# Four of the eight experts on 64 places each, with the low and the high part of a token side by side

## The chip, the core and the metric

The kernel runs on one core of a Trainium2 chip. TensorE (PE) multiplies, VectorE (DVE) and ScalarE (ACT) work on tiles, GpSimd (POOL) does little here, and SyncE (SP) issues the loads from HBM. The metric is the time of one execution on the device in microseconds; the median of three runs of the kernel before is 2383.63 us (2382.58 to 2390.08).

## The reference, cut to what matters

Two blocks of two layers each run over 256 tokens of width 1024. The last layer's feed-forward part is a mixture of eight experts, and it alone is touched by the change:

```python
logits = (t @ w_router) + b_router
top_v, top_i = lax.top_k(logits, 2)
top_w = softmax(top_v)
combine = sum(one_hot(top_i, 8) * top_w[..., None], axis=1)
for e in range(8):
    y += combine[:, e:e+1] * ((silu(t @ w1[e]) * (t @ w3[e])) @ w2[e])
```

w1 and w3 are 1024 x 2816, w2 is 2816 x 1024, all float32: 34.6 MB an expert. With the inputs as they are drawn (seed 0) the reference's router gives the eight experts 56, 59, 87, 61, 48, 82, 40 and 79 tokens, 512 in all.

## The kernel before

A float32 product is made from rounded parts: `split` (lines 417 to 419) lets ACT write the high part of a number (a cast) and DVE the low part (a subtraction), and `mm3` (lines 392 to 397) adds three products: high by high, high by low, low by high. Weights are loaded in units of 1 MB (128 x 2048) by `unit` and `raw` (lines 356 to 381) into a ring of five buffers, `raw`; each unit is then split in two halves of 128 x 1024 into `whi` (five buffers) and `wlo` (four). A load can start when both halves of the unit that held its buffer are split.

`moe` (line 1788) computes the router's logits, ranks the experts of a token, and counts on PE (lines 1841 to 1845) the place that a token takes in each of its two experts. `moe_round` (line 1877) then takes the experts in four pairs. For a pair it builds one-hot tiles `oh` from the places (line 1894), gathers the tokens of both experts with products by `oh` into `gh` and `gl` (high and low part, 128 places an expert), runs `expert` twice, and adds both results to the tokens through the transposed one-hot `ohT` (line 1928). This stretch between two experts of different pairs is called the boundary below.

`expert` (line 1932) goes over 11 blocks of 256 columns. A block takes three units: e1, e3 (eight row blocks of 128 x 256 each) and e2. It has 48 products of 256 columns into `ps_mm`, a SiLU on ACT, a product on DVE, two transposes, a split into `eph` and `epl`, and 12 products of 512 columns into `ps_acc`; the latter run one block late (`pend`).

All engines take their instructions in order, and a scheduler wrote that order from estimates of its own. If an expert had over 128 tokens, the code behind `tc.If` (line 1871) would run all experts once more.

Of the kernel before, what the change touches and what calls it, by code (L numbers as in the profile page):

```python
# [127 lines left out]
def _consts():  # L128
# [33 lines left out]
    c['tri8'] = np.broadcast_to(tri.reshape(1, 64), (P, 64))  # L162
    return {k: np.ascontiguousarray(v, dtype=np.float32).reshape(P, -1) for k, v in c.items()}
# [12 lines left out]
def pack(I):  # L176
# [30 lines left out]
    for e in range(NE):  # L207
        A[f'e1_{e}'] = _colblocks(I['exp_w1_2'][0, e])
        A[f'e3_{e}'] = _colblocks(I['exp_w3_2'][0, e])
        A[f'e2_{e}'] = _rowunits(I['exp_w2_2'][0, e])  # L210
# [74 lines left out]
class Kern:  # L285
# [1489 lines left out]
    def moe_consts(self, pw):  # L1775
        self.xw = pw
        self.pad(pw, 64)
        wr = pw.tile([P, KC * NE], F32, name="wr")
        self.nc.sync.dma_start(wr, self.a['wr'])
        lt = self.sm.tile([P, S], F32, tag="sq", bufs=2, name="ltf")[:, :P]  # L1780
        self.nc.sync.dma_start(lt, self.const_ap('lt'))
        ltb, oneb = pw.tile([P, P], BF, name="ltb"), pw.tile([P, P], BF, name="oneb")
        self.nc.vector.tensor_copy(ltb, lt)
        self.nc.vector.memset(oneb, 1.0)
        self.route = (wr, self.row(pw, 'brout'), self.c(pw, 'tri8'), ltb, oneb,
                      self.c(pw, 'iota'))

    def moe(self):
# [3 lines left out]
        with self.stage("moe") as pl:  # L1792
# [6 lines left out]
            wr, br, tri8, ltb, oneb, iota = self.route  # L1799
# [48 lines left out]
            tt(pos, pos, pp[:, 0:2 * NE].rearrange("p (t e) -> p t e", t=NT), op=ALU.add)  # L1848
            cnt = pl.tile([P, 1], F32, name="cnt")
            nc.vector.tensor_reduce(cnt, pp[:, 2 * NE:3 * NE], AX.X, ALU.max)  # L1850
# [16 lines left out]
            tiles = [tkh, tkl, pos, weights]  # L1867
            self.moe_round(pl, tiles, iota)
            self.final(pl)
            mx = nc.values_load(cnti[0:1, 0:1], min_val=0, max_val=S)  # L1870
            with tc.If(mx > P):

                ts(pos, pos, -float(P), None, op0=ALU.add)
                self.moe_round(pl, tiles, iota)
                self.final(pl)

    def moe_round(self, pl, tiles, iota):
# [5 lines left out]
        gate = self.mcol(1, 5, 0)  # L1883
        for e0 in range(0, NE, 2):
# [7 lines left out]
            for e in range(2):  # L1892
                for t in range(NT):
                    ts(oh[:, t, e], iota, pos[:, t, e0 + e:e0 + e + 1], None, op0=ALU.is_equal)
            gh = pl.tile([P, KC, 2 * P], F32R, tag="gh", name=self.nm("gh"))
            gl = pl.tile([P, KC, 2 * P], F32R, tag="gl", name=self.nm("gl"))
            for k in range(KC):
# [5 lines left out]
                nc.scalar.copy(gh[:, k], pg[:, 0:S])  # L1903
                nc.vector.tensor_copy(gl[:, k], pg[:, S:2 * S])
            if callable(tiles[3]):
                tiles[3] = tiles[3]()
            comb = tiles[3]
# [11 lines left out]
            ys = []  # L1919
            self.rings = [r for r in self.rings if r[0] is not self.xw and r[1] != "raw2"] + [(pl, "raw2", 1)]  # L1920
            for e in range(2):
                ys.append(self.expert(pl, e0 + e, (gh, gl), e, wsl[:, e:e + 1]))
            for m in range(KC):
                pm = self.psum("mx")
                n = 0
                for e in range(2):
                    for y in ys[e]:
                        nc.tensor.matmul(pm[:, :S], y[:, m * P:(m + 1) * P], ohT[:, e], start=n == 0, stop=n == 3)
                        n += 1
                self.resid(m, pm[:, :S], gate)  # L1930

    def expert(self, pl, e, g, t, wcol):
# [3 lines left out]
        def tail(fb, p):  # L1936
# [6 lines left out]
            w = self.blkunit(f'e2_{e}', fb, 2)  # L1943
# [6 lines left out]
        for fb in range(NF // 2):  # L1950
            w1 = self.blkunit(f'e1_{e}', fb, KC)
            pm = self.psum()
            self.proj_tm(pm[:, 0:256], w1, 0, 256, g, t)
            w3 = self.blkunit(f'e3_{e}', fb, KC)
# [7 lines left out]
        tail(*pend)  # L1962
        y = self.xw.tile([P, 2, D], F32R, tag=("xa", "xb")[t], name=self.nm("ey"))
# [58 lines left out]
```

## Time and profile before

| | |
|---|---|
| median of three runs | 2383.63 us |
| the profiled execution, and its span | 2392.68 us, 2390.8 us |
| busy in the span: PE, DVE, ACT | 2288.4, 1932.4, 1371.7 us |
| read from HBM | 515.55 MB, 216 GB/s over the span |
| loads of expert weights | 264 of 1 MB, the first issued at 1402.2 us, the last at 2335.8 us |

A view in stretches gives busy time by engine, with the number of instructions in brackets, the granted clock of TensorE (1.00 is 2.4 GHz), the busy share of the 16 DMA engines and the GB/s that they moved. In the order of time, a row of x3 is three instructions in one piece; its second number is the length of the whole piece. PE's instructions overlap: what one costs is the distance of starts, not its duration.

### The profile page before, as it was taken

The numbers are of one execution on the slowest core, as the hardware profiler recorded it, in microseconds if no ns is written. First come the engines' busy times: TensorE is split into PE (matmuls) and PEld (weight loads), VectorE is DVE, ScalarE is ACT, GpSimd is POOL, SyncE is SP. The second block draws the span as 40 slices with busy tenths as digits, with TensorE's granted clock in tenths as the row PEclk, the third lists the DMA queues.
The fourth block names the chain that finished last, engine by engine and source line by source line (L and its number), as shares of the span: only waits on it lengthen the run. The fifth ranks groups of instructions, "written<-read, shape, count | busy, mean of one in ns | idle before, by whom it ended". The sixth has DMA issues, their size and how long they took to land.

```text
span 2390.8 us, 41817 instructions
## 1 busy us (share of the span) xinstructions
PE 2288.4 (96%) x16477; PEld 2128.6 (89%) x16477; DVE 1932.4 (81%) x3447; ACT 1371.7 (57%) x2186; POOL 37.2 (2%) x40
## 2 busy tenths in 40 slices
PE   7999998999999999999999999989999999999998
PEld 7999998989998888888888898879999989999997
DVE  7879996768997886797657567779989998998996
ACT  6655554655544656432223246568877777876775
POOL 1000000000000000000000000000000000000000
PEclk9999998999998999999999999999999999999998
DMA  6335663534665231254655223269989998998992
GB/s 230 140 121 219 232 229 134 180 140 160 238 239 205 71 124 55 94 213 182 219 176 213 82 89 107 73 247 358 367 307 368 363 367 305 359 367 302 366 364 86
DMA packets 77453, 519.38 MB, mean 217 GB/s; under 512 B 10400, under 2 KB 12832, under 8 KB 15552
## 3 DMA queue, kind: packets, MB, share of 16 engines
q1 hardware_dynamic: 77248, 516.63, 58.9%
q8 instruction: 131, 2.15, 0.4%
q14 instruction: 74, 0.61, 0.1%
HBM read 515.55 MB, written 1.05 MB: 216 GB/s over the span
## 4 chain that ended last, share of the span: by engine, by line
PE 86%; DVE 8%; ACT 2%; issue 2%; DMA 2%; POOL 0%; SPq 0%; DVEq 0%; ACTq 0%; POOLq 0%
PE ps_mm L395 15%; PE ps_mm L396 15%; PE ps_mm L397 15%; PE ps_acc L395 7%; PE ps_acc L396 7%; PE ps_acc L397 7%; PE ps_mx L395 3%; PE ps_mx L397 3%; PE ps_mx L396 3%; DVE wlo L419 2%; PE ps_mx L472 2%; PE ps_acc L1532 1%; PE ps_acc L1355 1%; PE ps_mx L1901 1%; DMA raw<-wmod 1%
## 5 line engine op out<-in xcount | busy, mean ns | idle before, releaser
L418 ACT CAST whi<-raw 128x1024 fp32r<-128x1024 f32 x875 | 900.9, 1045 | 463.7 <-PE ps_mm L397 137.7
L419 DVE TENSOR_TENSOR wlo<-raw,whi 128x1024 fp32r<-128x1024 f32 x875 | 1047.9, 1214 | 138.0 <-ACT whi L418 49.0
L396 PE MATMUL ps_mm<-wlo,gh 128*128 128x256 f32 x1408 | 391.6, 279 | 4.1 <-DVE wlo L419 4.1
L395 PE MATMUL ps_mm<-whi,gh 128*128 128x256 f32 x1408 | 394.0, 280 | 0.0
L397 PE MATMUL ps_mm<-whi,gl 128*128 128x256 f32 x1408 | 390.5, 278 | 0.0
L396 PEld LDWEIGHTS ps_mm<-wlo,gh 128*128 128x128 f32 x1408 | 264.3, 188 | 11.0 <-DVE wlo L419 5.7
L397 PEld LDWEIGHTS ps_mm<-whi,gl 128*128 128x128 f32 x1408 | 265.3, 189 | 5.7
L395 PEld LDWEIGHTS ps_mm<-whi,gh 128*128 128x128 f32 x1408 | 264.4, 188 | 1.7
L395 PE MATMUL ps_mm<-hhi,whi 128*128 128x256 f32 (+2 forms) x544 | 154.7, 284 | 23.0 <-ACT whi L418 15.0
L397 PE MATMUL ps_mm<-hhi,wlo 128*128 128x256 f32 (+2 forms) x544 | 153.9, 283 | 2.2 <-DVE wlo L419 2.1
L396 PE MATMUL ps_mm<-hlo,whi 128*128 128x256 f32 (+2 forms) x544 | 153.6, 282 | 1.6 <-DVE hlo L424 1.1
L395 PE MATMUL ps_mm<-whi,hhi 128*128 128x256 f32 x480 | 139.0, 290 | 6.3 <-DVE rot L515 3.4
L396 PE MATMUL ps_acc<-wlo,eph 128*128 128x512 f32 x352 | 139.0, 395 | 0.0
L1071 DVE SCALAR_TENSOR_TENSOR raw<-raw,cond 128x1024 f32<-128x1024 f32 x96 | 115.9, 1219 | 28.3 <-DMA raw<-wmod 27.8
L396 PE MATMUL ps_mm<-wlo,hhi 128*128 128x256 f32 x480 | 137.4, 287 | 0.0
L397 PE MATMUL ps_mm<-whi,hlo 128*128 128x256 f32 x480 | 137.1, 287 | 0.0
L395 PE MATMUL ps_acc<-whi,eph 128*128 128x512 f32 x352 | 135.4, 403 | 1.5 <-ACT eph L418 1.5
L397 PE MATMUL ps_acc<-whi,epl 128*128 128x512 f32 x352 | 132.1, 397 | 0.0
L395 PEld LDWEIGHTS ps_mm<-hhi,whi 128*128 128x128 f32 (+2 forms) x544 | 100.2, 184 | 25.0 <-ACT whi L418 15.4
L397 PE MATMUL ps_acc<-hhi,wlo 128*128 128x256 f32 x368 | 104.3, 284 | 1.4 <-DVE wlo L419 1.4
L396 PE MATMUL ps_acc<-hlo,whi 128*128 128x256 f32 x368 | 104.2, 284 | 0.0
L395 PE MATMUL ps_acc<-hhi,whi 128*128 128x256 f32 x368 | 104.1, 284 | 0.0
(595 smaller groups left out, 5487.1 us busy)
## 6 DMA issues: line engine op xcount, KB each, us to landing
raw<-e SPq DMA_DIRECT2D x264, 1024.0 KB, 6.9
raw<-up SPq DMA_DIRECT2D x66, 1024.0 KB, 5.3
raw<-wmod SPq DMA_DIRECT2D x48, 1024.0 KB, 4.9
raw<-dn SPq DMA_DIRECT2D x33, 1024.0 KB, 4.9
raw<-win SPq DMA_DIRECT2D x27, 1024.0 KB, 4.9
raw<-w_odd SPq DMA_DIRECT2D x12, 1024.0 KB, 4.8
raw<-wout SPq DMA_DIRECT2D x12, 1024.0 KB, 4.9
raw<-w_even SPq DMA_DIRECT2D x10, 1024.0 KB, 5.0
```

Source lines behind the costliest of these rows:

```text
L395: mm(out, st[0], mv[0], start=start, stop=False, **kw)
L396: mm(out, st[0], mv[1], start=False, stop=False, **kw)
L397: mm(out, st[1], mv[0], start=False, stop=stop, **kw)
L418: self.nc.scalar.copy(hi, src)
L419: self.nc.vector.tensor_tensor(lo, src, hi, op=ALU.subtract)
L472: self.nc.tensor.transpose(out, in_, self.ident[:k, :k])
L1071: stt(w[:, j], w[:, j], 0.5, self.cond[0], op0=ALU.mult, op1=ALU.mult, accum_out=m[:, j, 0:1])
L1355: nc.tensor.matmul(po[0][:, t * 64:t * 64 + 64], pT[:, kt], v, start=kt == 0, stop=kt == nk - 1)
L1532: nc.tensor.matmul(o, x1, x2, start=n == 0, stop=n == len(terms) - 1)
L1901: nc.tensor.matmul(pg[:, a * S:(a + 1) * S], src[:, t, k * P:(k + 1) * P], oh[:, t].rearrange("p e n -> p (e n)"), start=t == 0, stop=t == ...
```

## The change

The experts are ranked on chip by their number of tokens. Expert 0 always takes the second place of the first pair, so that its loads need no ranking. Of the other seven the four with the fewest tokens become the first of the four pairs, the larger ones the second; `turns` holds which rank stands at which place. A pair runs its second expert first. Weights of experts other than 0 are loaded from an address that SP reads from SBUF (`whoi`).

The small expert has 64 places. Its one-hot repeats 64 places twice, and `gh` then holds the low parts in 64 columns and the high parts in the next 64, so that one stationary tile of 128 rows carries both. It is multiplied by `whi` and by `wlo`: two products instead of three. Products by `pick` (the identity's two halves added, an old tile) add the two parts and transpose at once. If the small four exceed 64 tokens or the others 128, a full round follows, as before.

```diff
+            ca = pl.tile([P, NE], F32, name="ca")
+            nc.vector.tensor_copy(ca, pp[:, 2 * NE:3 * NE])
+            nc.vector.memset(ca[:, 0:1], -1.0)
+            g8, at, e8 = gt[:, 0], gt[:, 1], eq[:, 0]
+            mine, other = ca[:, :, None].to_broadcast([P, NE, NE]), ca[:, None, :].to_broadcast([P, NE, NE])
+            tt(g8, other, mine, op=ALU.is_lt)
+            tt(e8, other, mine, op=ALU.is_equal)
+            tt(e8, e8, tri8, op=ALU.mult)
+            tt(g8, g8, e8, op=ALU.add)
+            rk = pl.tile([P, NE], F32, name="rk")
+            nc.vector.tensor_reduce(rk, g8, AX.X, ALU.add)
+
+            tt(at, rk[:, None, :].to_broadcast([P, NE, NE]), turns.rearrange("p (a b) -> p a b", a=NE), op=ALU.is_equal)
+
+            def byturn(out, x):
+                tt(e8, at, x[:, None, :].to_broadcast([P, NE, NE]), op=ALU.mult)
+                nc.vector.tensor_reduce(out, e8, AX.X, ALU.add)
+            posr = pl.tile([P, NT, NE], F32, name="posr")
+            for t in range(NT):
+                byturn(posr[:, t], pos[:, t])
...
+            def expert(i):
+                if i == 1:
+                    return 0
+                return nc.values_load(whoi[0:1, i:i + 1], engines=(mybir.EngineType.SP,), min_val=0, max_val=NE - 1)
...
+                    nc.scalar.copy(gh[:, k, 64:2 * P], pg[:, 64:S])
+                    nc.scalar.copy(gh[:, k, 0:64], pg[:, S:S + 64])
+                    nc.vector.tensor_copy(gl[:, k, P:2 * P], pg[:, S + P:2 * S])
...
+            for e in (1, 0) if small else (0, 1):
+                at = expert(e0 + e) if small else e0 + e
+                if small and e == 0:
+                    ys[e] = self.expert64(pl, at, gh, e, wsl[:, e:e + 1])
...
+    def eunit(self, name, e, i, k):
+        ap = self.a[name]
+        ap = ap[e, i] if isinstance(e, int) else ap[bass.ds(e, 1), i].rearrange("o p n -> p (o n)")
+        return self.unit(ap, k, 2048 // k)
...
+        def turn(a):
+            pt = self.psum("mx")
+            for i in range(4):
+                mm(pt[:, i * 64:i * 64 + 64], a[i // 2][:, i % 2 * P:i % 2 * P + P], pick, start=True, stop=True)
+            s = pl.tile([P, P], F32, tag="es", bufs=2, name=self.nm("es"))
+            nc.scalar.activation(s, pt[:, 0:P], AF.Silu)
+            nc.vector.tensor_tensor(s, s, pt[:, P:2 * P], op=ALU.mult)
+            ph = pl.tile([P, 2, P], F32R, tag="eph", bufs=2, name=self.nm("eph"))
+            self.split(ph[:, :, 64:P], ph[:, :, 0:64], s.rearrange("p (a b) -> p a b", a=2))
+            return ph
...
+                    for n, x in enumerate(w(j, half * 512, half * 512 + 512)):
+                        mm(py[half], ph[:, j], x, start=fb == 0 and j == 0 and n == 0,
+                           stop=fb == NF // 2 - 1 and j == 1 and n == 1)
...
+                for k in range(KC):
+                    for n, x in enumerate(w(k, 0, 256)):
+                        mm(o, gs[:, k, 0:P], x, start=k == 0 and n == 0, stop=k == KC - 1 and n == 1)
+                a.append(pl.tile([P, 256], F32, tag=("ep", "epl")[i], bufs=2, name=self.nm("ea")))
+                nc.scalar.copy(a[i], o)
+            if held:
+                down(*held)
+            held = (fb - 1, turn(up)) if up else None
```

On DVE, between a token's place (`pos`) and the first one-hot tile (`oh`), before:

```order
L1848 TENSOR_TENSOR pos<-pos,ps_mx_17047 128x16
L1850 TENSOR_REDUCE cnt<-ps_mx_17047 128x1
L1862 TENSOR_REDUCE dn<-ex 128x2
L1894 TENSOR_SCALAR oh_17061<-iota_11755,pos 128x128 x2
L1852 CAST cnti<-cnt 128x1
```

and after (`gt` and `eq` hold comparisons of counts, `rk` the rank, `posr` the places in the new order):

```order
L1852 COPY ca<-ps_mx_17049 128x8
L1895 TENSOR_REDUCE dn<-ex 128x2
L1853 MEMSET ca 128x1
L1896 RECIPROCAL dn<-dn 128x2
L1856 TENSOR_TENSOR gt<-ca 128x64
L1857 TENSOR_TENSOR eq<-ca 128x64
L1898 TENSOR_TENSOR comb<-ex,dn 128x16
L1858 TENSOR_TENSOR eq<-eq,tri_1916_11753 128x64
L1859 TENSOR_TENSOR gt<-gt,eq 128x64
L1861 TENSOR_REDUCE rk<-gt 128x8
L1863 TENSOR_TENSOR gt<-rk,turns_11757 128x64
L1876 TENSOR_SCALAR cap<-rk 128x8
```

Then follow a product and a sum (lines 1866 and 1867) and another product before the first `oh` (line 1946): fifteen instructions stand where two stood.

On ACT, one block of an expert before (`whi` casts of six halves, the SiLU `ep`, the cast `eph`):

```order
L1957 ACTIVATE ep_19957<-ps_mm_19898 128x256
L418 CAST whi_20026<-raw_20024 128x1024
L418 CAST whi_20030<-raw_20024 128x1024
L418 CAST whi_20070<-raw_20068 128x1024
L418 CAST whi_20074<-raw_20068 128x1024
L418 CAST whi_20092<-raw_20090 128x1024
L418 CAST whi_20096<-raw_20090 128x1024
L1957 ACTIVATE ep_20058<-ps_mm_19999 128x256
```

and one block of a small expert after (`ea` copies of the products of e1 and e3, `es` the SiLU):

```order
L2046 ACTIVATE es_23318<-ps_mx_23313 128x128
L419 CAST whi_23269<-raw_23267 128x1024
L419 CAST whi_23273<-raw_23267 128x1024
L419 CAST eph_23321<-es_23318 128x2x64
L2071 COPY ea_23265<-ps_mm_23238 128x256
L419 CAST whi_23297<-raw_23295 128x1024
L419 CAST whi_23301<-raw_23295 128x1024
L2071 COPY ea_23293<-ps_mm_23238 128x256
L419 CAST whi_23327<-raw_23325 128x1024
L419 CAST whi_23331<-raw_23325 128x1024
L2046 ACTIVATE es_23404<-ps_mx_23399 128x128
```

Two copies that wait for PE now stand between the casts, and in front of the first of them the SiLU, two casts and the cast of `eph`. On SP, behind the twelve loads of expert 0 that are issued ahead of the routing, before:

```order
L380 DMA raw_17527<-e_0 128x2048
L380 DMA raw_17325<-e_0 128x2048
L1870 TENSOR_LOAD cnti
L1870 ISA x2
L380 DMA raw_17562<-e_0 128x2048
```

and after:

```order
L381 DMA raw_17568<-e 128x2048
L381 DMA raw_17366<-e 128x2048
L1915 TENSOR_LOAD whoi
L1915 ISA x2
...
L1918 TENSOR_LOAD cnti
L1918 ISA x2
L381 DMA raw_17603<-e 128x2048
```

Where one reading of a number stood, seven of `whoi` and one of `cnti` stand, in front of the rest of expert 0's loads.

## Rows read from the trace of the kernel before

**Rows 1.** The page's 40 slices: busy tenths of PE and DMA.

```profile
PE   7999998999999999999999999989999999999998
...
DMA  6335663534665231254655223269989998998992
```

**Rows 2.** Busy time by engine in two stretches, columns as headed.

```profile
core 0: us, PE busy (x) PEld busy (x) DVE busy (x) ACT busy (x) POOL busy (x), PEclk, DMA share, GB/s
...
1600.00:1700.00 100.00, 99.51 (x725) 93.05 (x724) 91.71 (x96) 79.99 (x95) 0.00 (x0) 1.00 0.97 365
...
1700.00:1800.00 100.00, 97.95 (x719) 91.40 (x718) 89.22 (x108) 73.54 (x95) 0.00 (x0) 1.00 0.88 329
```

**Rows 3.** Groups by shape, 1600 to 1700 us: xcount, busy us, mean ns.

```profile
L395 PE MATMUL ps_mm<-whi,gh 128*128 128x256 f32 x188 | 52.5, 279 | 0.0
...
L396 PE MATMUL ps_acc<-wlo,eph 128*128 128x512 f32 x47 | 18.6, 395 | 0.0
...
L419 DVE TENSOR_TENSOR wlo<-raw,whi 128x1024 fp32r<-128x1024 f32 x71 | 85.0, 1221 | 8.1 <-ACT whi L418 4.8 <-PE ps_mm L396 0.2
...
L418 ACT CAST whi<-raw 128x1024 fp32r<-128x1024 f32 x71 | 73.8, 1051 | 17.4 <-PE ps_mm L397 14.1 <-PE ps_acc L397 2.6
...
L1958 DVE TENSOR_TENSOR ep<-ep,ps_mm 128x256 f32<-128x256 f32 x12 | 5.0, 412 | 0.0
...
L418 ACT CAST eph<-ps_mx 128x256 fp32r<-128x256 f32 x11 | 4.1, 371 | 0.0
```

**Rows 4.** PE in order of time: start, duration.

```profile
1781.87 0.28 PE L397 MATMUL ps_mm<-whi,gl 128*128 128x256 f32 x1
...
1782.89 0.28 PE L397 MATMUL ps_mm<-whi,gl 128*128 128x256 f32 x1
...
1761.82 0.40 PE L396 MATMUL ps_acc<-wlo,eph 128*128 128x512 f32 x1
...
1762.75 0.40 PE L397 MATMUL ps_acc<-whi,epl 128*128 128x512 f32 x1
...
1770.83 0.74 PE L1928 MATMUL ps_mx<-ohT,ey 128*128 128x256 f32 x4 [0.74 <-DVE ey L424]
...
1971.17 0.74 PE L1928 MATMUL ps_mx<-ohT,ey 128*128 128x256 f32 x4 [0.74 <-DVE ey L424]
```

**Rows 5.** DVE and ACT in order of time, three halves in one piece.

```profile
1691.38 3.49 DVE L419 TENSOR_TENSOR wlo<-raw,whi 128x1024 fp32r<-128x1024 f32 x3
...
2359.91 3.03 ACT L418 CAST whi<-raw 128x1024 fp32r<-128x1024 f32 x3 [1.21 <-PE ps_mm L397]
```

**Rows 6.** SP's waits, 1600 to 1700 us; the page's expert loads.

```profile
SPq L380 <- DVE wlo L419: 59.7, 23, 3.2
...
raw<-e SPq DMA_DIRECT2D x264, 1024.0 KB, 6.9
```

**Rows 7.** Three stretches of 10 us, columns as in Rows 2.

```profile
1600.00:1610.00 10.00, 10.00 (x81) 9.64 (x80) 9.34 (x10) 8.31 (x10) 0.00 (x0) 1.00 0.97 401
...
1750.00:1760.00 10.00, 10.00 (x79) 9.55 (x78) 8.69 (x11) 7.51 (x10) 0.00 (x0) 1.00 1.01 415
...
1770.00:1780.00 10.00, 8.95 (x74) 8.66 (x74) 8.37 (x19) 4.22 (x10) 0.00 (x0) 1.00 0.45 164
```

**Rows 8.** Routing: DVE in order of time, PE's gather in the chain.

```profile
1568.92 0.29 DVE L1832 TENSOR_REDUCE rank<-gt 128x16 f32<-128x128 f32 x1
...
1569.88 0.17 DVE L1848 TENSOR_TENSOR pos<-pos,ps_mx 128x16 f32<-128x16 f32 x1
...
1570.12 0.47 DVE L1894 TENSOR_SCALAR oh<-iota,pos 128x128 fp32r<-128x128 f32 x2
...
1570.99 3.55 PE ps_mx L1901 x16
```

**Rows 9.** SP: a number read from SBUF, and the next load.

```profile
L1870 SPq TENSOR_LOAD <-cnti x1: 470/470/470, 1570.8 to 1570.8; - x1
...
1582.74 0.34 SPq L380 DMA_DIRECT2D raw<-e  x1
```

More of the change, by code (lines that the diff above doesn't have):

```diff
@@ L1866, in weights, with comb, moe_round @@
                 return comb
-            tiles = [tkh, tkl, pos, weights]
-            self.moe_round(pl, tiles, iota)
+            combs = []
+            def comb():
+                if not combs:
+                    c = weights()
+                    combs.append(c)
+                    r = pl.tile([P, NT, NE], F32, name="combr")
+                    for t in range(NT):
+                        byturn(r[:, t], c[:, t])
+                    combs.append(r)
+                return combs[1]
+            def expert(i):
+                if i == 1:
+                    return 0
+                return nc.values_load(whoi[0:1, i:i + 1], engines=(mybir.EngineType.SP,), min_val=0, max_val=NE - 1)
+            self.moe_round(pl, [tkh, tkl, posr, comb], iota, expert)
             self.final(pl)
             mx = nc.values_load(cnti[0:1, 0:1], min_val=0, max_val=S)
-            with tc.If(mx > P):
-                ts(pos, pos, -float(P), None, op0=ALU.add)
-                self.moe_round(pl, tiles, iota)
+            with tc.If(mx > 0):
+                tt(pos, pos, cap[:, None, :].to_broadcast([P, NT, NE]), op=ALU.subtract)
+                self.moe_round(pl, [tkh, tkl, pos, combs[0]], iota)
                 self.final(pl)
-    def moe_round(self, pl, tiles, iota):
+    def moe_round(self, pl, tiles, iota, expert=None):
         nc = self.nc
@@ L1883, in moe_round @@
         gate = self.mcol(1, 5, 0)
+        small = expert is not None
         for e0 in range(0, NE, 2):
@@ L1891, in moe_round @@
             ohT = pl.tile([P, 2, S], F32R, tag="ohT", name=self.nm("ohT"))
[L1892 to L1894 removed]
+            for t in range(NT):
+                for e in range(2):
+                    p = pos[:, t, e0 + e:e0 + e + 1]
+                    if small and e == 0:
+                        ts(oh[:, t, 0].rearrange("p (a n) -> p a n", a=2), iota[:, None, 0:64].to_broadcast([P, 2, 64]), p,
+                           None, op0=ALU.is_equal)
+                    else:
+                        ts(oh[:, t, e], iota, p, None, op0=ALU.is_equal)
             gh = pl.tile([P, KC, 2 * P], F32R, tag="gh", name=self.nm("gh"))
@@ L1918, in moe_round @@
             nc.vector.tensor_copy(wsl, pw[:, 0:2])
-            ys = []
+            ys = {}
             self.rings = [r for r in self.rings if r[0] is not self.xw and r[1] != "raw2"] + [(pl, "raw2", 1)]
-            for e in range(2):
-                ys.append(self.expert(pl, e0 + e, (gh, gl), e, wsl[:, e:e + 1]))
+            for e in (1, 0) if small else (0, 1):
+                at = expert(e0 + e) if small else e0 + e
+                if small and e == 0:
+                    ys[e] = self.expert64(pl, at, gh, e, wsl[:, e:e + 1])
+                else:
+                    ys[e] = self.expert(pl, at, (gh, gl), e, wsl[:, e:e + 1])
             for m in range(KC):
@@ L1925, in moe_round @@
                 n = 0
-                for e in range(2):
+                for e in ys:
                     for y in ys[e]:
```

62 lines of the change are left out of this document (47 added, 15 removed).

## Prediction

> **What bounds the kernel now.** I read the page's 40 slices first: from about slice 27 to the end PE and the DMA engines are both at 9 of 10 [rows 1]. That stretch is the experts, and two things that are full at once are what the change has to get past, so the next view is the busy time by engine in stretches. From 1600 to 1700 us, inside a pair, PE is busy 99.51 of 100 us, the DMA share is 0.97 at 365 GB/s, DVE is busy 91.71 us and ACT 79.99 [rows 2]. The reader should see four resources within 20% of each other, PE first.
>
> The groups by shape give the block. 188 products of high by high in that stretch, 16 to a block, are 11.75 blocks in 100 us: 8.51 us a block, 93.6 us an expert of 11 blocks. PE's starts confirm that it is PE: products of 256 columns start (1782.89 - 1781.87) / 9 = 0.113 us apart, those of 512 columns (1762.75 - 1761.82) / 4 = 0.233 us [rows 4], so 48 and 12 of them make 5.44 + 2.79 = 8.23 us, and two transposes and the changes between them the rest. The same place of two boundaries lies 1971.17 - 1770.83 = 200.3 us apart [rows 4]: a pair is two experts of 93.6 us and a boundary of 13.1 us. In the boundary the DMA share falls to 0.45 [rows 7], since the ring is full and nothing frees it.
>
> Who waits for whom: SP spends 59.7 of those 100 us waiting for a buffer that DVE's low part frees [rows 6]. So the loads follow PE through the ring today; the 365 GB/s is what PE asks for, not shown to be the most that they can do.
>
> **The change part by part.** One block of a small expert, resource by resource.
>
> PE: 32 products of 256 columns by 0.113 us are 3.63 us, eight of 512 columns by 0.233 us 1.86 us; four products of 64 columns are not in the trace and are put at no more than one of 256 columns each, 0.45 us. Sum 5.9 us, 2.6 less than 8.51. PE no longer sets the block.
>
> DVE: six low parts. Back to back they start (3.49 - 1.22) / 2 = 1.14 us apart [rows 3, 5]: 6.81 us. Its two other operations shrink from 256 to 128 columns. From 1221 ns at 1024 columns and 412 ns at 256 [rows 3] a column costs 1.05 ns, so 128 columns take 0.28 us, some 0.08 of it overlapped as above: 0.25 us each. Sum 7.3 us.
>
> ACT: six casts, (3.03 - 1.05) / 2 = 0.99 us apart [rows 3, 5]: 5.94 us. Two copies of 256 columns are new, by the cast of 256 columns 0.37 us each [rows 3]; SiLU and cast of 128 columns come to 0.26 us by the same slope. Sum 7.2 us.
>
> Loads: three of 1,048,576 bytes. At the best rate of a 10 us stretch, 415 GB/s [rows 7], one takes 2.53 us and a block 7.6; at the mean of 365 GB/s 2.87 us and 8.6. I take the better end, because of these rows: with five buffers PE alone decides when a load may start, two stretches of 10 us reach 401 and 415 GB/s, and a small expert begins with a full ring and can take that lead along.
>
> On this point the Trainium skill is against the change: the page "DMA: Bandwidth & Descriptors", section "Where 436 GB/s comes from", says that for loads from HBM to SBUF a limit of about 358 GB/s for a core binds. By that figure, as an estimate, a load would take 2.93 us, a pair of 66 loads not under 193 us instead of 200.3, and the sum below would be about -25 us. The trace does not agree where it matters, with 415 GB/s over 10 us and 365 over 100 [rows 2, 7].
>
> So DVE, ACT and the loads stand at 7.3, 7.2 and 7.6 us. I take 7.6 us a block: the loads' term, which is also DVE's with 0.3 us for the waits between engines that follow each other closely. A small expert is 11 x 7.6 = 83.6 us, 10.0 less than 93.6.
>
> Its end is worth less. The last block's chain (copies, turn, SiLU, product, split) is covered by the products of the block before, which shrink from 12 to 8 of 512 columns: 4 x 0.233 = 0.9 us of cover is gone. Ends: 0 if other work stands there, 2 us if the copies also wait. I take 0.9 us.
>
> The large expert keeps its code and PE its 8.51 us. In the boundary the gather keeps its 32 products a part; ACT has two copies in place of one, DVE half of each `gl`; PE works on the next expert's first block between the gathers, so I count nothing there, up to 1 us if ACT's second copy (0.2 us by the slope, eight times) ends last. By the order, the transposes and weights of the slots stand where they stood.
>
> Routing is on the path. DVE writes `pos` at 1569.88 and the first `oh` at 1570.12, PE's first gather follows at 1570.99 and PE has nothing else [rows 8]. The change puts nine or ten dependent steps between the two. A dependent step took 0.24 us there (1569.88 to 1570.12) and, on 128 columns, at most 0.32 us (the sum of 0.29 us and its hand-over) [rows 8]: 9 x 0.24 = 2.2 to 10 x 0.32 = 3.2 us, I take 2.8.
>
> SP: reading a number took 0.47 us [rows 9]; with the two register instructions behind each I put it at 0.75 us, so eight take 6 us from when `whoi` is there, about 1575, to 1581. Queued behind are the remaining loads of expert 0 and all later ones; DVE's splits and PE would wait for them. Today the next load behind the reading goes out at 1582.74 [rows 9], held by its buffer, and with the routing 2.8 us later it would go at 1585.5. So it is covered; without that cover it would cost up to 6 us, once. A load by a register address has one more register instruction; SP has 2.5 us a load.
>
> Sum: four small experts, 4 x (10.0 - 0.9) = 36.4 us less; routing 2.8 us more: -33.6 us. The profiled execution, 2392.68 us, would come to 2359.1. The median is 9.05 us under it, and I put the same difference on it: 2350.0 us. The bounds: at DVE's 7.3 us a block and no loss at the ends 4 x 13.3 - 2.2 = 51 us less, 2333; at today's 8.51 us, 2 us at each end and 3.2 + 6 us for routing and SP, 17 us more, 2401.
>
> **Rivals.**
>
> *The loads set the pair.* For: the DMA share is already 0.97 [rows 2], and at 365 GB/s a pair's 66 loads take 189.4 us. If half of the boundary's idle DMA time stays (about 5 us), a pair is 194 us, 6 less: 4 x 6 less 2.8 is -21 us, 2362. Against: the stretches over 400 GB/s. Chance 0.21. The rule of the Trainium skill quoted above is this rival with 358 in place of 365 GB/s.
>
> *DVE's floor.* The splits run back to back, the lead of the ring and of `wlo` carries the loads, and the ends are covered: 2333 to 2340. Against: three resources within 4% of each other rarely run without gaps. Chance 0.12.
>
> *Nothing comes back.* Loads at their mean rate with today's idle time in the boundary: the block stays near 8.5 us, and routing and ends leave +3 to +7 us, 2387 to 2390. Chance 0.06.
>
> *ACT's copies hold up the casts (slower).* Place: ACT's queue in a small expert, where each of the two copies waits until PE is done with a unit, and the casts of the next unit stand behind it. By the order 2.5 us of other work (SiLU, two casts, `eph`) stand between a unit's last cast and its copy; DVE's low part (1.22 us) and eight products (0.91 us) need 2.1. If DVE comes later by one low part, each copy waits about 0.8 us, and what it holds comes later for DVE again. From 0.65 us of wait a copy (7.2 + 2 x 0.65 = 8.5) nothing is gained; at 1.14 us a block is 9.5 us, an expert 104.5, and the sum 4 x (10.9 + 0.9) + 2.8 = 50 us more, 2434. Against: whi has five buffers and can run ahead. Chance 0.05.
>
> *PE's clock falls.* PE would be busy 5.9 of 7.6 us in a small expert, 78%. The rows show a granted clock of 1.00 (2.4 GHz) at 99.5% and at 8.95 of 10 us [rows 2, 7], none at 78%. At 1.2 GHz PE would need 11.8 us a block: 130 us an expert, 2383.6 + 4 x 37 + 2.8, about 2534. Its gaps here are short. Chance 0.01.
>
> *The change does not hold.* If one of the small four had over 64 tokens or another over 128, all experts would run again, some 800 us more. The reference's counts, 40, 48, 59, 61 and then 79, 82, 87, with 56 for expert 0, leave it a chance of 0.01.
>
> **How the numbers follow.** The forecast has 0.54, on its own range 2341 to 2361, and the rivals 0.21, 0.12, 0.06, 0.05, 0.01 and 0.01. From 2334 to 2376 lie the forecast, most of the first rival (0.19) and half of the second: 0.79. A difference of under 0.3%, 7.2 us, can't be told from no change here. Faster: 0.54 + 0.12 + 0.20 = 0.86; the same: 0.06 and the rest of the first rival, 0.07; slower: 0.07.
>
> **What would show it.** In the profile after: in a 100 us stretch of a small expert PE below 85% busy, DVE above 93%, the DMA rate above 385 GB/s, and a new block every 7.6 us; the large experts unchanged at 8.51 us; a pair near 191 us; the first gather 2.8 us later than `pos` allows today; no wait of SP at the readings that a split waits for. I am wrong if ACT's idle time before a copy is over 0.5 us, if the DMA rate stays at 365 GB/s in a small expert, or if PE's starts there are 0.22 us apart.

## The result, and the profile after

The changed kernel takes 2355.2 us (median of four runs, 2351.5 to 2360.0) against 2385.2 us of the kernel before beside it: a ratio of 0.9872, 95% interval 0.9856 to 0.9888, or 30 us less. A second set of rounds gave 0.9876 (0.9853 to 0.9899). The forecast was 2350 and 33.6 us less.

The two profiled spans differ by 41.1 us (2390.8 and 2349.7), and not all of that is the change: the router's logits, before which nothing was changed, were written at these times, before and after.

```profile
1567.53 0.17 DVE L1811 TENSOR_TENSOR lg<-ps_mm,row 128x16 f32<-128x16 f32 x1 [0.88 <-PE ps_mm L472]
```

```profile
1560.15 0.17 DVE L1812 TENSOR_TENSOR lg<-ps_mm,row 128x16 f32<-128x16 f32 x1 [1.15 <-PE ps_mm L473]
```

So 7.4 us lie in unchanged code. In the other runs below the same instruction stands anywhere from 1554.9 to 1568.1 us. What the change did is read from the logits to the end: 823.3 us before, 789.5 after, 33.8 us less, and 792.2 in the repeated profile.

The pairs start with PE's first gather. Three of these starts before and three after (start, duration; the first ones are at 1570.99 [rows 8] and, below, 1565.62):

```profile
1773.82 0.40 PE L1901 MATMUL ps_mx<-oh,tkh 128*128 128x256 f32 x2
...
1974.16 0.40 PE L1901 MATMUL ps_mx<-oh,tkh 128*128 128x256 f32 x2
...
2174.66 0.40 PE L1901 MATMUL ps_mx<-oh,tkh 128*128 128x256 f32 x2
```

```profile
1757.74 0.40 PE L1956 MATMUL ps_mx<-oh,tkh 128*128 128x256 f32 x2
...
1949.13 0.50 PE L1956 MATMUL ps_mx<-oh,tkh 128*128 128x256 f32 x2 [0.62 <-DVE xT L805]
...
2141.83 0.50 PE L1956 MATMUL ps_mx<-oh,tkh 128*128 128x256 f32 x2 [0.60 <-DVE xT L805]
```

The first three pairs take 192.1, 191.4 and 192.7 us instead of 202.8, 200.3 and 200.5; the last one, to the end of the span, 207.8 instead of 216.2. That is 10.7, 8.9, 7.8 and 8.3 us less, where the forecast had 9.1 for each. Routing takes 2.0 us of it back. DVE and PE there, in answer to [rows 8]:

```profile
1562.50 0.17 DVE L1849 TENSOR_TENSOR pos<-pos,ps_mx 128x16 f32<-128x16 f32 x1
...
1565.00 0.28 DVE L1946 TENSOR_SCALAR oh<-iota,posr 128x128 fp32r<-128x128 f32 x1
...
1565.97 0.28 DVE L1949 TENSOR_SCALAR oh<-iota,posr 128x128 fp32r<-128x128 f32 x1
```

```profile
1565.62 1.26 PE L1956 MATMUL ps_mx<-oh,tkh 128*128 128x256 f32 x4 [3.17 <-DVE posr L1867]
```

From `pos` to the first `oh` it is 2.50 us now, 0.24 before; but the gather starts when the one-hots of the first 128 tokens stand, so PE lost 2.0 us from the logits on (5.47 against 3.46) and not 2.8. The readings of SP are covered, as the forecast had it: seven at 0.26 to 0.47 us (one took 0.47 before [rows 9]), done at 1570.9, an eighth done at 1571.5, and the next load goes out at 1578.42, when a buffer comes free:

```profile
L1915 SPq TENSOR_LOAD <-whoi x7: 262/262/473, 1566.7 to 1570.4; - x7
```

```profile
1578.42 11.79 SPq L381 DMA_DIRECT2D raw<-e  x5
```

Busy time by engine in the small experts of pairs 1, 2 and 3, in answer to [rows 2]:

```profile
core 0: us, PE busy (x) PEld busy (x) DVE busy (x) ACT busy (x) POOL busy (x), PEclk, DMA share, GB/s
1710.00:1740.00 30.00, 27.74 (x195) 24.48 (x194) 29.44 (x35) 27.63 (x41) 0.00 (x0) 1.00 1.01 419
1904.00:1934.00 30.00, 27.16 (x185) 23.60 (x185) 28.13 (x32) 25.33 (x38) 0.00 (x0) 1.00 1.00 399
2090.00:2120.00 30.00, 27.34 (x184) 23.88 (x184) 27.46 (x31) 25.49 (x38) 0.00 (x0) 1.00 0.99 391
```

The large experts are as before: their SiLUs come 8.24 and 8.80 us apart in turn in both kernels, 8.52 on average. The small ones are not alike: in pair 1 DVE is busy 98% at 419 GB/s, in pairs 2 and 3 94% and 92% at 399 and 391. ACT's SiLU `es` comes once a block, and its distances tell the rest: in pair 1 the steady block is 7.45 to 7.49 us, in pairs 2 to 4 7.90 to 8.01, nearly always 7.92. None of the four begins steadily. These are the first two SiLUs of pair 2, 6.53 us apart; the next distances are 5.83, 6.14, 4.70 and 7.02:

```profile
1866.21 0.31 ACT L2046 ACTIVATE es<-ps_mx 128x128 f32<-128x128 f32 x1
...
1872.74 0.28 ACT L2046 ACTIVATE es<-ps_mx 128x128 f32<-128x128 f32 x1
```

The granted clock is 1.00 in the stretches above, but at the ends of the small experts of pairs 1 and 3 it stood at 1.2 GHz for 3.4 us. PE had worked with gaps before that, in pair 1 1.77 of 4 us (columns as above):

```profile
1747.00:1751.00 4.00, 1.77 (x9) 1.29 (x8) 2.85 (x5) 2.53 (x4) 0.00 (x0) 1.00 1.01 416
1751.40:1754.80 3.40, 3.37 (x12) 2.37 (x10) 3.19 (x4) 2.92 (x4) 0.00 (x0) 0.50 1.02 424
```

In the first gather products of 256 columns start 0.21 us apart while the clock is at 0.50 and 0.12 us apart at 1.00, so, as an estimate, each fall costs up to 1.7 us. The kernel before and the run with the ranks alone show no such stretch between the first gather and the end of the last expert, the other kernels one to four.

Why 7.92 us and not 7.5 is to be seen in one steady block of pair 2, on ACT (the next SiLU is at 1912.26) and then on DVE (start, duration, in brackets the idle time before it and who ended it):

```profile
1904.35 0.27 ACT L2046 ACTIVATE es<-ps_mx 128x128 f32<-128x128 f32 x1
1904.51 1.99 ACT L419 CAST whi<-raw 128x1024 fp32r<-128x1024 f32 x2
1906.40 0.30 ACT L419 CAST eph<-es 128x128 fp32r<-128x128 f32 x1
1907.06 0.37 ACT L2071 COPY ea<-ps_mm 128x256 f32<-128x256 f32 x1 [0.36 <-PE ps_mm L2069]
1907.33 2.00 ACT L419 CAST whi<-raw 128x1024 fp32r<-128x1024 f32 x2
1910.09 0.38 ACT L2071 COPY ea<-ps_mm 128x256 f32<-128x256 f32 x1 [0.77 <-PE ps_mm L2069]
1910.36 2.00 ACT L419 CAST whi<-raw 128x1024 fp32r<-128x1024 f32 x2
```

```profile
1903.53 2.36 DVE L420 TENSOR_TENSOR wlo<-raw,whi 128x1024 fp32r<-128x1024 f32 x2 [0.61 <-ACT whi L419]
...
1911.45 2.36 DVE L420 TENSOR_TENSOR wlo<-raw,whi 128x1024 fp32r<-128x1024 f32 x2 [0.61 <-ACT whi L419]
```

Both copies wait for PE, 0.36 and 0.77 us; the cast behind the second one comes late, and DVE stands 0.61 us for it. PE in its turn waits for the copies, as the waits of 30 us in pair 3 say (total us, times, longest):

```profile
ACT ea L2071 <- PE ps_mm L2069: 4.5, 8, 0.8
...
PE ps_mm L2069 <- ACT ea L2071: 1.8, 4, 0.5
```

The products of e3 go into the other half of the tile that the first copy reads, so they are ordered behind it. In the block above (L2044 are four products of `turn`):

```profile
1907.48 0.38 PE L2069 MATMUL ps_mm<-whi,gh 128*128 128x256 f32 x1 [0.46 <-ACT ea L2071]
...
1908.62 0.55 PE L2044 MATMUL ps_mx<-pick,ea 128*128 128x64 f32 x4
1908.99 0.36 PE L2069 MATMUL ps_mm<-wlo,gh 128*128 128x256 f32 x1
```

No engine is full and the loads are not at their best rate: a loop of hand-overs ACT, DVE, PE, ACT sets the block. It can be followed once around: the two low parts of e1 on DVE (1903.53 to 1905.89), the products of e1's second half on PE (to 1907.02), the first copy (to 1907.43), all products of e3 with the four of `turn` among them (to 1910.06), the second copy, a cast of the next e1 (to 1911.41), and the next low part at 1911.45, 7.92 us after 1903.53. No step starts more than 0.05 us after the one before it is done.

The order on ACT says why ACT waits. In pairs 2 to 4 only two casts (2.0 us) stand between the copies, and e3's products take 2.6 us. In pair 1 the order is another one, with the copies between single casts, and in 30 us there (1710 to 1740) ACT waits far less:

```profile
ACT ea L2071 <- PE ps_mm L2069: 0.7, 2, 0.4
```

### The profile page after: what moved, and what is told of

It is laid out like the page before. It is cut to its first block, busy times and chain, and to the rows that moved or that the text cites. A ratio compares the mean times of both kernels' runs of the same rounds, so it can differ in the third digit from the quotient of the medians.

```text
span 2349.7 us, 41203 instructions
## 1 busy us (share of the span) xinstructions
PE 2216.4 (94%) x15861; PEld 2044.7 (87%) x15861; DVE 1911.2 (81%) x3472; ACT 1376.6 (59%) x2306; POOL 37.2 (2%) x40
## 5 line engine op out<-in xcount | busy, mean ns | idle before, releaser
L397 PE MATMUL ps_mm<-wlo,gh 128*128 128x256 f32 x704 | 195.1, 278 | 2.3 <-DVE wlo L420 2.3
L396 PE MATMUL ps_mm<-whi,gh 128*128 128x256 f32 x704 | 197.0, 280 | 0.0
L398 PE MATMUL ps_mm<-whi,gl 128*128 128x256 f32 x704 | 195.4, 278 | 0.0
L2069 PE MATMUL ps_mm<-whi,gh 128*128 128x256 f32 x704 | 174.4, 285 | 14.5 <-ACT ea L2071 11.2
L2069 PE MATMUL ps_mm<-wlo,gh 128*128 128x256 f32 x704 | 177.4, 290 | 6.3 <-DVE wlo L420 6.3
L398 PEld LDWEIGHTS ps_mm<-whi,gl 128*128 128x128 f32 x704 | 132.8, 189 | 2.6
```

The lines of the kernel that those rows point to most:

```text
L396: mm(out, st[0], mv[0], start=start, stop=False, **kw)
L397: mm(out, st[0], mv[1], start=False, stop=False, **kw)
L398: mm(out, st[1], mv[0], start=False, stop=stop, **kw)
L2069: mm(o, gs[:, k, 0:P], x, start=k == 0 and n == 0, stop=k == KC - 1 and n == 1)
```

## The experiments

All ratios are to the kernel before, with 95% intervals; 0.001 is 2.4 us. "From the logits" is the time from that instruction to the end in the profile (after: 789.5 and 792.2). An expert's time "from split to split" runs from ACT's last split of the result of the expert before it to that of its own. The edits are shown cut to what matters.

**Ranks alone.**

```diff
-                if small and e == 0:
-                    ys[e] = self.expert64(pl, at, gh, e, wsl[:, e:e + 1])
-                else:
-                    ys[e] = self.expert(pl, at, (gh, gl), e, wsl[:, e:e + 1])
+                ys[e] = self.expert(pl, at, (gh, gl), e, wsl[:, e:e + 1])
```

(`oh`, `gh` and `gl` are made as before, too.)

> Ranks, the new order of the experts and the addresses from a register stay; all eight experts keep 128 places and three products. It prices the routing and the addresses alone. My theory: the routing costs 2.0 to 2.8 us (in the trace after, the first gather comes 2.0 us later behind the logits than before) and the addresses nothing, so the kernel comes out at 2387 to 2388, 32 us behind the change, every expert at 92.6 us from end to end of its split. Rival: the addresses from a register slow the loads, or the new order of the pairs costs something at the boundary; then it is 2392 or more, and the stretch of a pair over 201 us.

Measured: 2387.3 us, ratio 1.0005 (0.9992 to 1.0018); from the logits 826.4 us, 3.1 more than before; experts at 92.6 to 92.7 us from split to split. As the theory had it: the routing costs little more than PE's first gather shows, and the rest of the change earns all of the gain. Of the 3.1 us the later gather is 2.0, and 0.8 more lie in the first pair (203.6 against 202.8 us). The granted clock fits that: it is 0.50 from 1563.9 to 1570.7 us here, with the gather starting at 1566.07, and 0.51 from 1570.7 to 1574.1 before, with the gather at 1570.99 [rows 8], so 4.6 us of it instead of 3.1 run at 1.2 GHz. The change has the same (0.50 until 1570.5, gather from 1565.62).

**Late copies.**

```diff
+            for i in range(2):
                 a.append(pl.tile([P, 256], F32, tag=("ep", "epl")[i], bufs=2, name=self.nm("ea")))
-                nc.scalar.copy(a[i], o)
+                nc.scalar.copy(a[i], pm[:, 256 * i:256 * i + 256])
```

> In a small expert both copies of a block are written behind the products of e3, instead of one behind e1 and one behind e3; nothing else. In the trace after, the steady blocks of pairs 2 to 4 take 7.92 us: ACT waits 0.36 and 0.77 us a block for PE before its copies, PE 0.46 us for the first copy, DVE 0.61 us for a cast, and no one is full. My theory: these copies hold the casts there, and loads could come every 2.49 us. Then the steady block comes to 7.5 us in pairs 2 to 4 (loads' 3 x 2.49, DVE's 7.3) and stays at 7.5 in pair 1: about 20 blocks by 0.4 us, 5 to 9 us less than the change. Rival: the loads give no more than 397 GB/s in these pairs (three in 7.92 us), or DVE is the floor; then the steady block stays at 7.9 us and the time within 2 us of the change.

Measured: 2338.6 us, ratio 0.9799 (0.9783 to 0.9815), some 18 us under the change; from the logits 777.9 us, 12 to 14 less. The same place on ACT in pair 3, and the busy time in that stretch (columns as above):

```profile
2098.95 0.65 ACT L2072 COPY ea<-ps_mm 128x256 f32<-128x256 f32 x2 [0.87 <-PE ps_mm L2069]
```

```profile
2090.00:2120.00 30.00, 29.44 (x190) 24.46 (x189) 28.67 (x33) 26.50 (x41) 0.00 (x0) 1.00 1.01 420
```

The two copies wait once, 0.87 us instead of 1.13, PE's products of e3 no longer wait for a copy, the steady block is 7.63 us in pairs 2 to 4 (the theory had 7.5) and the loads come at 420 GB/s. The theory holds against its rival: 391 to 399 GB/s were not a limit. A loop is there still, but it runs over DVE now, from e1's low parts through those of e3 (2092.95 to 2097.77), then eight products, the copies and a cast. The gain is larger than 5 to 9 us: the steady blocks make some 4 us of it (15 by 0.29), and much of the rest is in the blocks ahead of them, which got shorter too.

**One low part less.**

```diff
+            if nolow and a:
...
+                nc.scalar.copy(hi, raw[:, a:a + m])
+                halves.append((hi, halves[0][1]))
+                continue
```

> In a small expert the low part of the second half of e3's unit is left out, and PE takes the first half's in its place: part of the computation is wrong, the products are as many. DVE has 6.2 us of work a block instead of 7.3; ACT's order in the steady blocks is as in the change. My theory: in pairs 2 to 4 the chain cast, low part, product, copy sets the block, and it gets shorter by up to 1.1 us; the loads then hold at 3 x 2.49 = 7.47 us, in pair 1 they do already. So 7.92 falls to 7.5 us in pairs 2 to 4 and pair 1 stays at 7.47: 5 to 10 us less than the change. Rival 'DVE is the floor everywhere': blocks fall to 7 us or less in pair 1 too, 20 us less or more. Rival 'loads at 397 GB/s': nothing changes, 7.92 us stay.

Measured: 2335.1 us, ratio 0.9794 (0.9776 to 0.9812), 19 us under the change; steady blocks 7.42 to 7.45 us in pairs 2 to 4. Busy time in pair 2, columns as above:

```profile
1900.00:1930.00 30.00, 27.71 (x183) 24.39 (x183) 26.26 (x30) 27.00 (x40) 0.00 (x0) 1.00 1.01 419
```

The block fell from 7.92 to 7.44 as expected, at 419 GB/s, but the rows give another reason than the theory. The low part that is gone was not on the loop: in the change e3's low parts are done at 1908.36, and PE comes to the second half of e3 at 1908.99. What got shorter is PE's run of e3, since the order on PE moved with the edit: the products of `turn` now stand behind those of e3 (1905.77 to 1907.87), and no longer among them.

```profile
1905.77 0.38 PE L2074 MATMUL ps_mm<-whi,gh 128*128 128x256 f32 x1 [0.46 <-ACT ea L2076]
...
1907.70 0.55 PE L2049 MATMUL ps_mx<-pick,ea 128*128 128x64 f32 x4
```

That is 2.10 us instead of 2.58, the whole difference of 0.48 us, and the loop closes as before, with the copies waiting 0.36 and 0.29 us. So in pairs 2 to 4 this run shows the loop again, and not what a low part on DVE is worth. In pair 1 it was not as expected: its blocks, 7.5 before, now go up and down between 4.7 and 7.9 us, and this expert takes 75.1 us from split to split instead of 82.1. It lives on the lead of the loads to its end: by the landing times a load is 17 us ahead of its first cast at the start of this expert and 9 to 10 at its end. It could not do so while DVE had 7.3 us of work a block.

**Half of e3's loads.**

```diff
+            self.split(hi, lo, raw[:, 0:m] if half else raw[:, a:a + m])
...
+        return self.unit(ap[:, 0:HALF] if half else ap, k, 2048 // k, half=half)
```

> In a small expert only the first half of e3's unit is loaded, and both halves of the work are done on it: half of e3 is left out of the computation, the work of PE, DVE and ACT is as before. A block loads 2.5 MB instead of 3. My theory: pairs 2 to 4 do not wait for loads, so their steady blocks stay at 7.9 us, or at what a shifted order of the copies makes of them, and the DMA share falls below 0.9; pair 1, which stands at the loads' floor of 7.47 us, can fall only to DVE's 7.3. So the time is 0 to 5 us below the change. Rival 'loads set the small experts': 2.5 loads by 2.64 us are 6.6 us, DVE's 7.3 us set the block, 0.6 us by 22 blocks or more, 12 to 16 us below the change, with DVE at 100%.

Measured: 2342.9 us, ratio 0.9815 (0.9798 to 0.9833), about 14 us under the change by the medians, 6 to 8 by the profiles. Busy time in pair 2:

```profile
1904.00:1934.00 30.00, 27.48 (x194) 24.42 (x194) 29.30 (x32) 28.28 (x41) 0.00 (x0) 1.00 0.98 379
```

This one does not tell the theories apart, since the order of the copies moved with the edit: all four small experts now have the one of pair 1, and all four have its steady block, 7.38 to 7.53 us. But it shows two things. A block of 7.48 us does not need the loads' limit, because here it loads 2.5 MB, which is 350 GB/s (the 379 of the row have loads of the next large expert in them). DVE is busy 29.30 of 30 us, so its 7.3 us of work are what sets this block, and the one of pair 1 in the change. And the share of DMA time, 0.98 here, says nothing of a limit: it is 0.97 at 365 GB/s before [rows 2], and 1.01 at 419.

**The change again; numbers written into the loads.**

```diff
-                return nc.values_load(whoi[0:1, i:i + 1], engines=(mybir.EngineType.SP,), min_val=0, max_val=NE - 1)
+                return (6, 0, 4, 7, 1, 5, 3, 2)[i]
```

> The changed kernel as it is, timed beside the kernels of this set. Its first four runs gave 2355.2 us; the stretch before the logits of the router, which the change does not touch, was 7.4 us shorter in its profile than in the profile of before, so the two profiles can't be subtracted as a whole. My theory: from the logits to the end it takes 789 to 791 us again (823.3 us before), with 7.9 us blocks in pairs 2 to 4 and 7.5 us in pair 1, and the median lies between 2350 and 2356. If blocks of 7.9 us turn up in pair 1 too, or 7.5 us in pairs 2 to 4, the order of the copies does not set them.

> The change with the numbers of the experts written into the loads (for these inputs they are known), so that SP reads none of the seven from SBUF and no load has an address from a register; the ranking on DVE stays but for the part that only makes those numbers. My theory: the readings are covered by the ring and a load by register costs nothing that anything waits for, so the time is within 2 us of the change. Rival: the seven readings (4.5 us on SP) or the addresses hold up loads; then it is 4 us less or more.

Measured: the change 0.9876 (0.9853 to 0.9899), from the logits 792.2 us, with the same blocks of 7.5 and 7.9 us in the same pairs; with fixed numbers 0.9868 (0.9845 to 0.9891), 790.9 us from the logits. That is no difference within these intervals (0.0023 is 5 us), and none in the profiles: the loads by a register cost nothing that can be seen here.

**Half of the loads and one low part less** (the two edits above together).

> In a small expert only the first half of e3's unit is loaded and both halves of the work are done on it, and the second half's low part is left out: part of e3 is left out of the computation, PE's and ACT's work is as before, loads are 2.5 MB a block and DVE has 6.2 us a block. With either edit alone a steady block came to 7.48 us (less loads) and 7.44 us (less low parts, DMA share 1.01 at 419 GB/s). My theory: with the loads whole, 3 x 2.48 = 7.44 us is their floor; with both edits neither loads (6.2 us) nor DVE (6.2 us) hold, and the block goes to ACT's own 6.8 us, up to 7.2 with its waits: the small experts about 4 us shorter each than with the low part alone. Rival: the 7.44 us came from the chain copy, product, copy between ACT and PE (ACT's work of 6.8 us and 0.65 us of waits); then the block stays at 7.4 us.

Measured: 2311.4 us, ratio 0.9705 (0.9685 to 0.9724). Busy time in pair 2:

```profile
1880.00:1910.00 30.00, 29.95 (x220) 28.16 (x219) 28.86 (x33) 30.00 (x46) 0.00 (x0) 1.00 1.01 410
```

SiLUs now alternate between 5.62 and 7.53 us, 6.57 us a block, and ACT is busy 30.00 of 30 us: ACT's own floor, below the 6.8 us expected. In pairs 2 and 3 a small expert takes 74.6 us from split to split, 4.6 to 4.8 less than with the low part alone. The 7.44 us were not ACT's work; the copies again stand elsewhere, so this run does not tell loads and loop apart.

**Five small experts, late copies.**

```diff
-            ts(cap, rk, 0.5, None, op0=ALU.is_gt)
-            ts(big, rk, 4.5, None, op0=ALU.is_lt)
-            tt(cap, cap, big, op=ALU.mult)
+            ts(cap, rk, 4.5, None, op0=ALU.is_lt)
...
-                if small and e == 0:
+                if small and (e == 0 or e0 == 0):
                     ys[e] = self.expert64(pl, at, gh, e, wsl[:, e:e + 1])
...
```

> Expert 0 works on 64 places too (56 tokens here), so five of eight experts have two products instead of three, and the copies are written behind e3 as in the second kernel of the first set. In the first pair both experts fill their 64 low and 64 high columns, so ACT has four copies a part of the first gather and DVE none. My theory: expert 0 gains what a small expert gains in late copies, 92.6 - 81 = 11 to 12 us less its end; up to 2 us come back at the first gather (two more copies of 0.3 us for each of eight parts). So 8 to 12 us less than late copies, about 2329. Rival: expert 0 starts behind the routing with an empty lead and its loads come late, or ACT's copies hold the first gather: then it is less than 5 us.

Measured: 2322.4 us, ratio 0.9747 (0.9731 to 0.9763), 12 us under late copies by the ratios. It beats both kernels, at a price: with over 64 tokens for expert 0 (56 here) all experts run once more.

**Copies on DVE.**

```diff
-                nc.scalar.copy(a[i], o)
+                nc.vector.tensor_copy(a[i], o)
```

> The two copies of a block in a small expert are made by DVE instead of ACT; nothing else. It gives ACT 0.7 us a block back and DVE 0.66 us more (128 x 256 from PSUM took DVE 0.41 us, 0.08 of it beside the next). My theory: DVE then is the floor, 7.3 + 0.66 = 7.97 us a block, in every small expert: pair 1 goes from 7.48 to 8.0 us, pairs 2 to 4 from 7.92 to 8.0: 4 to 8 us more than the change. Rival 'the copies hurt only because ACT's casts stand behind them': then with ACT freed the blocks fall below 7.9 us and the time is that of the change or less.

Measured: 2365.4 us, ratio 0.9918 (0.9903 to 0.9933), some 10 us over the change; steady blocks of 7.76 to 7.95 us in all four. Busy time in pair 2:

```profile
1900.00:1930.00 30.00, 26.47 (x183) 22.99 (x182) 30.00 (x39) 24.38 (x32) 0.00 (x0) 1.00 1.01 405
```

DVE at 30.00 of 30 us is the floor, as the theory said. The loss is above the 4 to 8 us expected: the short blocks at the start are gone (5.23, then 8.28 us), and small experts take 88 to 89 us from split to split (the last 85.3). The clock falls three times here, against two in the change.

**Five small experts, copies in place.** The edit of five small experts without late copies.

> Expert 0 on 64 places too, but the copies left where the change has them: it divides the 33.6 us that five small experts with late copies gain on the change. My theory: the two parts add up. Late copies were worth 17 us by the medians (12 to 14 us by the traces from the logits on) in four small experts, so this kernel stands 15 to 19 us under the change, about 2339, and its steady blocks are 7.5 or 7.9 us, depending on where its order puts the copies. Rival: late copies are needed for it, because five small experts share one order; then it gains less than 10 us.

Measured: 2344.0 us, ratio 0.983 (0.9815 to 0.9845): 10 to 11 us under the change, not 15 to 19. Expert 0 gained its 12.6 us (from the logits to its split 98.8 instead of 111.4), but the small expert of pair 2 now takes 86.8 instead of 82.9 us: its steady blocks begin after three short ones, in the change after five, and the clock falls at its end (at 1932 us). The gains do not add up, since an edit in one pair moves what the next one starts with.

**Small expert first in pairs 2 to 4.**

```diff
-            for e in (1, 0) if small else (0, 1):
+            for e in (1, 0) if small and e0 == 0 else (0, 1):
```

> In pairs 2 to 4 the small expert runs first and the large one second (the first pair keeps its order, since expert 0 is loaded ahead of the ranking). My theory: a small expert's first three or four blocks take 4.8 to 6 us instead of 7.9 because DVE and the loads are ahead of PE when it starts, and the boundary behind it fills that lead again while PE gathers: the DMA share there was 0.78 at 302 GB/s in the change, 0.45 at 164 GB/s before it. With the small expert first its own start keeps the lead, but the large expert behind it starts with none, and the boundary behind the large one finds a full ring: large experts 2 to 5 us longer, DMA share in the boundary 0.5 or less, 5 to 15 us more than the change. Rival: the large expert's own slack (8.5 us against 7.5) makes up for it at once; then the time is within 4 us of the change.

Measured: 2349.8 us, ratio 0.9856 (0.9837 to 0.9874); 787.2 us from the logits. The parts went as my theory said: large experts took 96.4, 97.6 and 94.6 us instead of 92.6, and 10 us of the boundary behind pair 2 had 106 GB/s, where the change, in the same stretch and behind a small expert, has 274 (columns as above; this kernel, then the change):

```profile
1945.00:1955.00 10.00, 9.03 (x75) 8.62 (x74) 7.96 (x21) 5.04 (x18) 0.00 (x0) 1.00 0.30 106
```

```profile
1945.00:1955.00 10.00, 8.29 (x65) 7.89 (x66) 7.82 (x17) 5.19 (x19) 0.00 (x0) 1.00 0.73 274
```

but the boundary with the small expert behind it takes 94.0 to 96.4 us instead of some 97 to 99 (82.9 to 84.3, and 108 less 93.6 for the boundary). The sum is the rival's, within 4 us of the change. The lead is moved, not lost.

**One low part less, late copies.**

> Late copies, and in a small expert the low part of the second half of e3's unit left out as in the third kernel of the first set (part of the computation is wrong, the loads are whole). It asks what held that kernel at 7.44 us a block: the loads (3 x 2.48 us at 419 GB/s) or the chain between ACT's copies and PE, which had just 0.65 us of waits there. My theory: the loads. With the copies behind e3 and DVE at 6.2 us nothing else needs 7.4, so the steady block stays at 7.44 to 7.48 us with 419 to 421 GB/s, and the engines wait for landings. Rival: the chain; then the steady block changes with the place of the copies, to below 7.3 us or above 7.55.

Measured: 2332.4 us, ratio 0.979 (0.9772 to 0.9808); steady blocks 7.34 to 7.44 us. Busy time in pair 3:

```profile
2080.00:2110.00 30.00, 29.42 (x197) 24.95 (x197) 25.37 (x29) 27.36 (x41) 0.00 (x0) 1.00 1.01 418
```

The place of the copies changed and the block hardly did, at 418 GB/s, so neither sign of the two theories decides. The rows do: ACT still waits 0.64 us a block for PE, no engine waits for a landing, and a loop closes again, over the low parts of e1 and the one of e3 (2082.83 to 2086.52), fifteen products (to 2088.56), the copies, a cast, and the next low part at 2090.22, 7.39 us after the first. The landing times in the traces exclude the loads: counted unit by unit in the order of the loads, no load of an expert lands less than 7.9 us before the first cast of its unit starts, in any of the kernels, and in this block the distance is 13 us. That three loads at 2.49 us make 7.47 us, within 1% of the loop, is chance. The best 10 us among the experts of eleven of the runs have 420 to 424 GB/s.

## Why the prediction was right, and where it was not

*The sum.* 33.6 us less were forecast; from the logits it is 33.8 in the first pair of profiles and 31.1 with the repeated one, by the rounds 30 (27 to 34). That the small experts earn it is shown by the ranks alone, which gain nothing.

*PE leaves the path, the small block is 7.6 us.* PE did leave the path, and the size was right: small experts take 82.1, 82.9, 84.2 and 84.3 us from split to split, forecast 83.6 and 0.9. The reason was not. I had one block length, set by the loads. In fact the first three to five distances of SiLUs are 5.6 to 6.2 us on average, which I put down to what DVE and the loads have done ahead, the steady ones 7.5 (pair 1, DVE's work) or 7.9 us (pairs 2 to 4, the loop), and the last one 8.1 to 8.6. That these errors nearly cancel is luck, and so is how close the sum came. The products of a turn stand as eight in the trace, 0.73 us a block and not the 0.45 put for them.

*Loads at 2.53 us.* They can: 2.49 us each, 419 GB/s over 30 us in pair 1. The rule of the Trainium skill that was weighed ("DMA: Bandwidth & Descriptors", "Where 436 GB/s comes from", about 358 GB/s) does not hold here; the rival that rested on 365 GB/s fell with it. But the loads, whose term the sum took for the block, set no small expert's block: they land 11 us or more ahead of their casts in the change. They can run so far ahead because the ring is not the five buffers that the text before the prediction and the prediction count. `raw` has four, and six tiles of other pools are added to it on the way (lines 1642, 1671, 1674 and 1920; those of line 1642's `xw` leave again): each load goes out right behind the second low part of the unit ten before it.

*DVE 7.3 us, ACT 7.2 us.* DVE's term holds (98% busy in blocks of 7.48 us; copies on DVE: 7.3 + 0.66 expected, 7.9 measured at 100% busy). ACT's was too high: 6.57 us when it is full.

*The rival "ACT's copies hold up the casts".* This is the step that failed. I set it aside because 2.5 us of other work stand between a unit's last cast and its copy. That holds by the order for both copies (for the second `eph`, the first copy and two casts, 2.7 us), but I did not count that PE starts e3's products only when the first copy is done. From there the second copy has two casts (2.0 us) to cover 2.6 us of products, and waits 0.77 us; the first waits 0.36. The waits, 0.57 us on average, stayed below the 0.65 us from which I had it decide: so it cost some 0.3 to 0.4 us a steady block in three of four small experts and did not turn the sign. Late copies give 12 to 14 us back by the profiles, 18 by the ratios.

*The rival "PE's clock falls".* Not in the blocks, where it is 1.00 with PE busy 91 to 92%, but at the ends of two small experts, for 3.4 us each, and for longer in the first gather. The sum had nothing for it; it is up to 3.4 us and about 0.8.

*End of a small expert, boundary.* Large expert and boundary together take 106.8 to 108.7 us from split to split, 107.7 to 107.9 before: nothing there, as forecast. What the end alone costs was not taken apart; the last distance of SiLUs is 0.6 to 0.7 us over the steady one, where 0.9 was put.

*Routing +2.8, readings covered.* 2.0 us until the gather, since it starts on the first one-hots, and 0.8 in it; ranks alone agrees. The readings (1566.7 to 1571.5, 4.8 us for eight where 6 were put) cost nothing, as fixed numbers show.

*Signs to look for.* DVE above 93%: 98 and 94, but 92 in pair 3. DMA above 385 GB/s: 391 to 419. PE below 85%: no, 91 to 92%. A product is 0.28 us long in the rows while the next can start 0.11 us after it [rows 3, 4], so short waits leave no idle time, and some lengthen the record (286 and 297 ns on average in pair 2 against 279). A new block every 7.6 us: no, 7.5 and 7.9. Large experts at 8.51: 8.52. A pair near 191 us: 191.4 to 192.7 for the first three. And one sign of being wrong came true: ACT's idle time before a copy is over 0.5 us, 0.57 on average in the steady blocks read in pairs 2 and 3. It pointed at the step that failed.

## What to carry to other kernels

When several resources stand within 5% of each other, what sets the block can be the hand-over between them, as it was here: write down, for every instruction that a chain waits for, what stands between it and its producer on its own queue, for each place it occurs in and not for the first one found. Read stages at their start and in their middle apart, since a stage behind one that was bound elsewhere can live on the lead for some blocks. Before a rate of loads is called the limit, look how long before its use each load lands. Where a copy reads one part of a PSUM tile and a product writes another, try the copy behind the product: here it gave 12 to 18 us.

## What the runs showed of the hardware that was not expected

Half of the change's expert loads landed 2.48 to 2.50 us behind the load before, and over stretches of 30 us one core read 418 to 420 GB/s from HBM. The DMA share stands at 0.97 to 1.01 for rates from 365 to 420 GB/s, so it did not tell how much was left. The granted clock fell to 1.2 GHz for 3.4 us at the end of two small experts, in pair 1 behind 4 us in which PE was busy 1.77.
